# Twelve modulation vectors of a two-block network made by GpSimd and ScalarE in the feed forwards, in place of TensorE

## The chip, the core and the metric

The kernel runs on one core of a Trainium2 chip. The metric is device time in microseconds. Engines are named as the profile names them: PE is TensorE's matmul, PEld its weight load, DVE is VectorE, ACT is ScalarE, POOL is GpSimd, SP issues most DMAs. Each engine runs its own instructions in the order in which the program emits them; semaphores order them across engines.

## What is computed

A latent stream of 512 tokens and a context stream of 256 tokens, 1024 features each, pass two layers of a first block (attention, then a feed forward; a gated linear recurrence, then a feed forward) and two layers of a second block. Every norm is modulated by vectors that depend on a conditioning alone, one conditioning for each stream:

```python
mod_lat = jnp.dot(jax.nn.silu(c), ada_w[layer]) + ada_b[layer]
mod_ctx = jnp.dot(jax.nn.silu(c_ctx), ada_w[layer]) + ada_b[layer]
sh1, sc1, gt1, sh2, sc2, gt2 = jnp.split(mod_lat, 6, axis=-1)
...
x = x + gt1 * out_lat
x = x + gt2 * conv_ffn(modulate(rmsnorm(x, norm2_g[layer]), sh2, sc2), ...)

def conv_ffn(h, w_up, conv_w, conv_b, w_down):
    gate, val = jnp.split(jnp.dot(h, w_up), 2, axis=-1)
    return jnp.dot(jax.nn.silu(dwconv(gate, conv_w, conv_b)) * val, w_down)
```

The second block has three such vectors a layer (`w_mod`). That is 18 vectors of 1024 features, for two streams each; each is a product of a conditioning of 1024 with a matrix of 1024 x 1024. In the last layer of each block the context isn't updated, and some vectors are needed for the latents alone.

## The kernel before

Features lie over the 128 partitions (8 tiles, `KT`), tokens along the free axis (768 columns: context 256, latents 512). All products are exact float32 products made of three single passes: an operand is split into a high part (ACT, `split`, L357 to L360) and a low part (DVE, L360 through `tt`, L346). Weights come in tiles of 128x1024 (`raw`, three buffers, SP, L383); `weight` (L400) hands out the parts of one tile, loads up to three ahead and splits one ahead (tiles `wh` and `wl`).

`blk` (L510) is one block: take a weight, multiply 8 K tiles in three passes (`lin`, L409), call `fill`, then `tick`, then queue the evacuation of this block. `later` (L429) queues a function for a later `tick`; functions due at the same tick run in the order of their third argument. So the evacuation of a block is emitted behind the products of the next one.

A feed forward (`ffn`, L898) runs over 22 pairs of up blocks (gate, value). The gate's evacuation is `put` (DVE from PSUM), `conv` (L844, one `tensor_scalar` and four `scalar_tensor_tensor`), a tanh on ACT and the SiLU product on DVE; the value's is a product from PSUM, one or two `scalar_tensor_tensor`, and the split of the result (tiles `ah`, `ahl`). After each group of 2 or 3 pairs, beginning one pair late, the down products follow: 8 output tiles, with a `fill` after every second one (L962). The feed forward of layer 0 has both streams, that of layer 1 the latents alone, so that its blocks are a third shorter.

Modulation vectors are queued as steps in `self.todo`: 8 steps a vector, one for each tile of 128 rows of the matrix. A step of `modvec` (L532) is four matmuls of 128x32 by 128x256 in float32 (two passes each) into one PSUM bank, from a tile `ada` of 512 KB (two buffers) that SP loaded two steps ahead. After the eighth step ACT evacuates the bank, PE turns it by two transposes (L555) and DVE adds the bias. `fill(n)` (L646) runs up to n queued steps if `self.quota` allows; `mod(name)` (L669) runs what is missing when a vector is wanted. `run` (L2309) sets the quota by stage: 24 steps in the first attention, 48 in feed forward 0, 24 in feed forward 1, 16 and 16 in the second block. POOL is used for sums of squares and some products in other stages, not in the middle of the feed forwards.

Of the kernel before, what the change touches and what calls it, by code (L numbers as in the profile page):

```python
# [30 lines left out]
WIDE = {2: 512, 3: 256}       # columns of a tile of the second weights, by the K tiles of a chunk  # L31
# [3 lines left out]
# ---------------------------------------------------------------- host layout  # L35
# [19 lines left out]


def _vec(v):
    """[n * 128] -> [128, n]."""
    return v.reshape(-1, 128).T

# [13 lines left out]
def _constants():  # L74
# [7 lines left out]
    for b in range(5):                      # 3..7: two 64-lane heads of a block  # L82
        m = np.zeros((128, 32))
        m[:64, 2 * b] = 1 / 64
        m[64:, 2 * b + 1] = 1 / 64
        s.append(m)
    for q in range(8):                      # 8..15: 96 lanes of a head
# [7 lines left out]
    for p in range(4):                      # 16..19: nope lanes of a pair of heads  # L95
# [4 lines left out]
    m = np.zeros((128, 32))                 # 20: shared rotary lanes of the keys  # L100
    m[:32, :8] = 1 / 96
    s.append(m)
    for q in range(4):                      # 21..24: all lanes into column q
        m = np.zeros((128, 32))
        m[:, q] = 1 / 128
        s.append(m)
# [5 lines left out]
    fold = np.zeros((128, 2))               # adds the rows 32 g + v over g  # L112
# [4 lines left out]
    cos, sin = _rope_angles(8)              # [32, 512]  # L117
# [5 lines left out]
    cos, sin = _rope_angles(16)             # [64, 512]  # L123
# [3 lines left out]
    low = np.where(i[None, :] <= i[:, None], 0.0, NEG)   # [t, s]: s <= t  # L127
# [17 lines left out]
def _prepare(inp):  # L145
    """Arrays of the launch: inputs laid out for the chip, and constants of the shapes."""
# [5 lines left out]
    o["ada"] = a["ada_w"]  # L152
    o["mod"] = a["w_mod_2"]
# [92 lines left out]
# ---------------------------------------------------------------- the program  # L246

ALLB = ((0, 0, 512), (512, 512, 258))        # (psum column, operand column, n); the last two are the shifts
# [3 lines left out]
ORDER = (6, 7, 4, 5, 0, 1, 2, 3)              # of the tiles of a merge  # L252
SC, SL = (0, NC), (NC, T)                    # column ranges of ctx and lat
# [3 lines left out]
class _Halves(list):  # L257
    """A weight tile in column halves: w[:, a:b] within one of them."""
# [8 lines left out]
class _Kernel:  # L267
    """The program in issue order: each engine runs its instructions in the order they are emitted."""

    def __init__(self, ctx, tc, I, at, out):  # L270
# [15 lines left out]
        self.quota, self.log = 0, False  # L286

    def split_psum(self, a, at=0):
        """Two tiles of two banks, and four of one bank or, for a == 3, a third large one and two;
        at: the place of the next large tile in their cycle, the third one the last."""  # L290
# [13 lines left out]
    # ---- tiles  # L304
# [26 lines left out]
    # ---- engines  # L331
# [4 lines left out]
    def logs(self):  # L336
        """The activation table that has the logarithm."""
# [19 lines left out]
    def split(self, hi, lo, x):  # L357
        """x as the sum of two parts that single passes carry."""
        self.act(hi, x)
        self.tt(lo, x, hi.bitcast(F32), ALU.subtract)  # L360

    def parts(self, t, c, name="hi"):
        """The two parts of t[:, c]."""
# [4 lines left out]
    # ---- weights, in the order of their use  # L368
# [31 lines left out]
    def weight(self, name, i):  # L400
        """The parts of the next weight tile; the following ones are loaded and split ahead."""
# [7 lines left out]
    def lin(self, w, xs, segs, off=0, stride=128):  # L409
        """psum[:, ...] = w^T x over the K tiles xs, three single passes a product."""  # L410
# [17 lines left out]
    # ---- work that follows a product once the next one is under way  # L428
# [17 lines left out]
    def lead(self, specs, h, segs, pre):  # L446
        """The first products of a phase, K tile by K tile as pre(k) makes the tiles; evacuated at once."""
# [21 lines left out]
    def pair(self, specs, xs, pre=None):  # L469
        """Two products side by side, their last K tiles at the end, or K tile by K tile behind pre."""  # L470
# [19 lines left out]
    def begin(self, specs, h, pre=None, streams=None):  # L490
        """The first two products of a phase; they are evacuated during the next one, when the inverse
        rms is there."""
# [25 lines left out]
    # ---- modulation vectors  # L518
    def cond(self, names, key):
        """silu of the two conditionings as a zero-padded stationary operand."""  # L520
# [9 lines left out]
        return S  # L530

    def modvec(self, name, S, w, c0, bias):  # L532
# [33 lines left out]
        for k in range(KT):  # L566
            self.todo.append((lambda k=k: load(k), lambda k=k: step(k)))

    def first_mods(self, S, w, c_sc, c_sh, b_sc, b_sh, g, h, consts, after):
        """Scale and shift of the first phase, feature tile by feature tile, and its scaled residual."""  # L570
# [75 lines left out]
    def fill(self, n=1):  # L646
        """n eighths of a pending vector, the loads two ahead."""
        def load():
            for i in range(min(self.ahead, len(self.todo))):
                if self.todo[i][0]:  # L650
                    self.todo[i][0]()
                    self.todo[i] = (None, self.todo[i][1])

        for _ in range(min(n, self.quota, len(self.todo))):
            self.quota -= 1
            load()
            self.todo.pop(0)[1]()
            load()

    def whole(self, flush=True):  # L660
        """Finish a vector that is under way."""
        if len(self.todo) % KT:
# [6 lines left out]
    def mod(self, name):  # L669
        while name not in self.mods:  # L670
            if name in self.coming:
# [6 lines left out]
    def gain(self, name, sc, g):  # L678
        """g * (1 + scale), per feature and stream."""
# [4 lines left out]
    # ---- norms  # L684
    def rows(self, ps, n):
        """[64, n] means -> their inverse roots."""
# [14 lines left out]
    def heads(self, ps, sel, sq, start, stop):  # L701
        """Means of heads into rows of two token halves."""
# [6 lines left out]
    def means(self, sqs, sel, streams):  # L709
        """Means over all lanes of the tiles: quarters of the tokens in partition groups, the same  # L710
        in each row of a group."""
# [8 lines left out]
    def root(self, ps, c0, n, load=True):  # L720
        """The inverse roots of means."""
# [10 lines left out]
    def refine(self, y, t, m, z):  # L732
        """y = m ** -0.5 with a Newton step."""
# [7 lines left out]
    def spread(self, R, f, streams=(0, 1)):  # L741
        """f(psum, stream, first column, end) with the token values spread over all lanes."""
# [10 lines left out]
    def rows_out(self, name, ps):  # L753
        """Inverse roots of heads, left in DRAM: [head, tokens]."""
# [7 lines left out]
    def row_in(self, d, rows):  # L762
        """The rows of one head, or of two heads over the lane halves, spread over the lanes."""
# [6 lines left out]
    def start(self, A, sh, lat=False):  # L770
        """State of a normalized, modulated residual: scaled residual and shift in parts, K tile by
        K tile; the inverse rms multiplies the products."""
# [23 lines left out]
    def accumulate(self, acc, x, c, alone=False):  # L796
        """Squares of x into the list of sums."""
# [7 lines left out]
    def arm(self, h, streams=None):  # L805
        """Inverse rms: the sums after the next product, the spread after the one behind it."""
# [16 lines left out]
    def put(self, ps, h, lat=None):  # L823
        """psum * rstd + shift product."""
# [6 lines left out]
    def scaled(self, ps, h, lat):  # L831
        """The terms of put: psum * rstd, shift product."""
# [6 lines left out]
    def times(self, out, t, b, y, lat):  # L839
        """(t + b) * y."""  # L840
# [3 lines left out]
    def conv(self, src, w, b, lat):  # L844
        """Three taps along the tokens of each stream."""
# [8 lines left out]
    def silu2(self, x, c):  # L854
        """2 * silu, in place."""
# [1544 lines left out]
```

## Time and profile before

| | |
|---|---|
| time, median of 3 runs | 2530.7 us (2529.43 to 2530.71) |
| span of the profiled execution | 2526.1 us |
| PE / PEld | 97% / 81% of the span |
| DVE / ACT / POOL | 61% / 39% / 9% |
| mean granted clock of TensorE | 0.989 of full speed |
| DMA | 238.55 MB, 94 GB/s in the mean |

The time includes a few microseconds around the span. PE's busy time includes the tails of pipelined matmuls, so it is read here by the spacing of starts. A line such as L346 or L343 is a helper that many places call; the names of the tiles (output, then inputs) tell which place it is. An instruction's record begins when its engine takes it up; where it then waits for something inside the chip, the wait is part of its duration.

### The profile page before, as it was taken

Reading aid. Unit: us, or ns where it says so; the run is one execution under the profiler, and the core shown is the slowest. Engines: PE = TensorE matmul, PEld = TensorE weight load, DVE = VectorE, ACT = ScalarE, POOL = GpSimd, SP = SyncE. Lnnn points to the kernel's source line nnn. Section 1 sums busy time; section 2 is a strip of 40 time slices with the busy share of each in tenths; the row PEclk is TensorE's granted clock in tenths of the full one; section 3 lists DMA queues with packets and bytes.
Section 4 is the critical chain, followed back from the end, with each engine's and each line's share of the span. In section 5 each row is a group of like instructions: output and inputs, shape, how many; then the busy total and the mean of one; then the engine's idle time right before and its main releaser. Section 6 shows DMA issues by size and latency. Waiting matters only on the chain.

```text
span 2526.1 us, 40542 instructions
## 1 busy us (share of the span) xinstructions
PE 2456.3 (97%) x16338; PEld 2049.2 (81%) x16338; DVE 1551.3 (61%) x2736; ACT 973.2 (39%) x2217; POOL 215.4 (9%) x149
## 2 busy tenths in 40 slices
PE   7998999999999999998999999999999999989998
PEld 5776666887888888887889888999878778879797
DVE  4436876556555656667666566666745575266764
ACT  4226666322121222243445422333432473344563
POOL 2001232100000000012110100000110000130001
PEclk9999999999999999998999999999999999999999
DMA  8441110124334322113121255332223202333012
GB/s 284 151 152 46 32 63 30 61 90 142 120 122 126 109 83 76 53 57 109 59 80 62 81 196 167 99 95 97 86 95 134 76 2 84 101 105 101 18 47 88
DMA packets 82731, 238.55 MB, mean 94 GB/s; under 512 B 10032, under 2 KB 22256, under 8 KB 82544
## 3 DMA queue, kind: packets, MB, share of 16 engines
q1 hardware_dynamic: 82256, 235.90, 29.0%
q8 instruction: 129, 2.11, 0.4%
q14 instruction: 58, 0.48, 0.1%
q10 hardware_dynamic: 288, 0.07, 0.0%
HBM read 233.27 MB, written 2.66 MB: 93 GB/s over the span
## 4 chain that ended last, share of the span: by engine, by line
PE 88%; DVE 6%; ACT 2%; DMA 2%; issue 1%; POOL 0%; SPq 0%; DVEq 0%; ACTq 0%; POOLq 0%
PE A L355 71%; PE B L355 14%; PE B L1077 3%; DMA ada<-in_ada_dram 1%; DVE sm L1066 1%; DVE wl L346 1%; DVE kf L346 1%; ACT P L334 0%; DVE conv L343 0%; DVE hl L343 0%; ACT wh L334 0%; DMA stsel<-in_stat_dram 0%; ACT hh L334 0%; DVE y L346 0%; DMA raw<-in_w_in_dram 0%
## 5 line engine op out<-in xcount | busy, mean ns | idle before, releaser
L355 PE MATMUL A<-hh,wh 128*128 128x258 f32 (+2 forms) x2704 | 646.5, 320 | 13.1 <-ACT hh L334 3.8
L355 PE MATMUL A<-hl,wh 128*128 128x258 f32 (+2 forms) x2704 | 631.1, 315 | 2.9 <-DVE hl L343 2.9
L346 DVE TENSOR_TENSOR wl<-raw,wh 128x512 fp32r<-128x512 f32 (+2 forms) x546 | 377.1, 713 | 417.1 <-ACT wh L334 401.8
L355 PE MATMUL A<-hh,wl 128*128 128x258 f32 (+2 forms) x2704 | 630.3, 314 | 0.0
L334 ACT ACTIVATE wh<-raw 128x512 fp32r<-128x512 f32 (+2 forms) x546 | 318.8, 604 | 567.8 <-PE A L355 399.7
L355 PEld LDWEIGHTS A<-hh,wh 128*128 128x128 f32 x2704 | 419.3, 190 | 75.0 <-issue 13.9
L355 PEld LDWEIGHTS A<-hl,wh 128*128 128x128 f32 x2704 | 419.2, 190 | 36.5 <-DVE hl L343 4.1
L355 PEld LDWEIGHTS A<-hh,wl 128*128 128x128 f32 x2704 | 419.3, 190 | 33.3
L346 POOL TENSOR_TENSOR sq<-sq 128x768 f32<-128x768 f32 (+2 forms) x45 | 65.5, 1454 | 1204.4 <-ACT sq L334 599.7
L334 ACT ACTIVATE P<-A,sm 128x768 f32<-128x768 f32 (+3 forms) x176 | 127.9, 727 | 97.1 <-DVE sm L1066 91.3
L355 PE MATMUL A<-ah,wh 128*128 128x512 f32 (+1 forms) x528 | 163.1, 363 | 1.2 <-DVE x L343 1.1
L355 PE MATMUL A<-ah,wl 128*128 128x512 f32 (+1 forms) x528 | 159.7, 357 | 0.0
L355 PE MATMUL A<-ahl,wh 128*128 128x512 f32 (+1 forms) x528 | 159.3, 356 | 0.0
L1066 DVE TENSOR_REDUCE sm<-A 128x1 f32<-128x768 f32 (+3 forms) x176 | 129.2, 734 | 45.0 <-PE A L355 44.2
L343 DVE SCALAR_TENSOR_TENSOR x<-A,gt2h,x 128x512 f32<-128x512 f32 x192 | 119.7, 655 | 43.4 <-PE A L355 43.3
L1077 PE MATMUL B<-ident,P 128*128 128x128 f32 x768 | 124.7, 287 | 7.6 <-DVE pt L1080 2.5
L1077 PEld LDWEIGHTS B<-ident,P 128*128 128x128 f32 x768 | 84.0, 143 | 51.3 <-issue 21.6
L334 ACT ACTIVATE th<-conv 128x768 f32<-128x768 f32 (+1 forms) x52 | 38.4, 739 | 221.1 <-DVE conv L343 221.1
L343 DVE SCALAR_TENSOR_TENSOR conv<-put,small,conv 128x511 f32<-128x511 f32 (+1 forms) x168 | 110.3, 670 | 5.0
L355 PEld LDWEIGHTS A<-ah,wh 128*128 128x128 f32 x528 | 86.8, 188 | 26.9 <-issue 4.6
L346 DVE TENSOR_TENSOR put<-A,rbc 128x768 f32<-128x768 f32 (+1 forms) x111 | 93.2, 840 | 21.4 <-ACT sm L334 21.3
L355 PE MATMUL B<-ada,S 128*32 128x256 f32 x1152 | 91.3, 397 | 9.1 <-DMA ada<-in_ada_dram 8.9
(356 smaller groups left out, 3328.9 us busy)
## 6 DMA issues: line engine op xcount, KB each, us to landing
raw<-in_w_up_dram SPq DMA_DIRECT2D x88, 512.0 KB, 3.3
raw<-in_w_in_dram SPq DMA_DIRECT2D x81, 512.0 KB, 3.9
ada<-in_ada_dram SPq DMA_DIRECT2D x80, 512.0 KB, 4.1
ada<-in_mod_dram SPq DMA_DIRECT2D x48, 512.0 KB, 3.9
raw<-in_w_dn_dram SPq DMA_DIRECT2D x48, 384.0 KB, 3.2
raw<-in_w_o_dram SPq DMA_DIRECT2D x24, 512.0 KB, 4.3
ada<-in_ada_dram SPq DMA_DIRECT2D x16, 384.0 KB, 8.0
raw<-in_w_dn_dram SPq DMA_DIRECT2D x8, 512.0 KB, 5.7
```

The costliest lines, as they stand in the source:

```text
L334: return self.nc.scalar.activation(out, in_, f, **k)
L343: return self.nc.vector.scalar_tensor_tensor(out, x, sc, y, op0=op0, op1=op1)
L346: return (e or self.nc.vector).tensor_tensor(out, x, y, op=op)
L355: return self.nc.tensor.matmul(out, l, r, start=start, stop=stop)
L1066: nc.vector.tensor_reduce(g.nm[:, z], u.ps[:, cols], axis=AX.X, op=ALU.max, negate=True)
L1077: nc.tensor.transpose(ps[:, 128 * i:128 * i + 128], u.P[:, c:c + 128], self.ident)
```

## The change

Six vectors of layer 1 of the first block (`sc1`, `sh1`, `gt1`, `sc2`, `sh2`, `gt2`) and all six of the second block are made by a new `modrow` in place of `modvec`. The matrices are stored transposed, so that a tile has 128 output features over the partitions and the 1024 inputs along the free axis. The conditioning is written once to DRAM (four DMAs of S's columns, behind the first attention), and loaded back as a row spread over all partitions. A step multiplies the tile by the row on POOL (`tensor_tensor`, once for each stream that needs the vector), and ACT sums along the free axis with `accum_out`. With two streams the first product goes to a spare tile and the second is made in place; with one it is made in place.

```diff
+    def rows_of(self, key):
+        if self.rowt is None:
+            self.rowt = [None, [self.pt(n=D) for _ in range(2)], self.pt(n=D)]
+        if self.rowt[0] != key:
+            self.rowt[0] = key
+            for v in range(2):
+                self.nc.sync.dma_start(self.rowt[1][v], self.sd[key][v:v + 1].to_broadcast([128, D]))
+        return self.rowt[1:]
+
+    def modrow(self, name, key, w, n, bias):
+        nc, st = self.nc, {}
+        def load(k):
+            st[k] = self.pw["ada"].tile([128, 1024], F32, tag="ada", name="ada")
+            nc.sync.dma_start(st[k], w[k])
+        def step(k):
+            rows, spare = self.rows_of(key)
+            if k == 0:
+                st["m"] = self.const("m_" + name, [128, KT, 2])
+                if n == 1:
+                    nc.gpsimd.memset(st["m"], 0.0)
+            m, raw = st["m"], st.pop(k)
+            outs = [spare, raw][2 - n:]
+            for v, o in enumerate(outs):
+                self.tt(o, raw, rows[v], ALU.mult, nc.gpsimd)
+            self.pending = True
+            def sums():
+                for v, o in enumerate(outs):
+                    self.act(o, o, accum_out=m[:, k, v:v + 1])
+                self.pending = False
+                if k == KT - 1:
+                    self.tt(m[:, :, 0:n], m[:, :, 0:n], bias..., ALU.add, nc.gpsimd)
+                    self.mods[name] = m
+            self.later(sums, 1, 3)
```

The sums are queued for the next `tick` with the third argument 3, so they are emitted behind the evacuations due at that tick. While such a step is pending, `fill` doesn't begin another and doesn't load ahead; a `fill` runs one such step at most. While the row tiles exist, `split` makes the low part by another DVE instruction:

```diff
     def split(self, hi, lo, x):
         self.act(hi, x)
-        self.tt(lo, x, hi.bitcast(F32), ALU.subtract)
+        if self.rowt:
+            self.stt(lo, x, 1.0, hi.bitcast(F32), ALU.mult, ALU.subtract)
+        else:
+            self.tt(lo, x, hi.bitcast(F32), ALU.subtract)
```

In `fill`, and in `run`:

```diff
             for i in range(min(self.ahead, len(self.todo))):
-                if self.todo[i][0]:
-                    self.todo[i][0]()
-                    self.todo[i] = (None, self.todo[i][1])
+                f, g, row = self.todo[i]
+                if f and not (row and i and self.pending):
+                    f()
+                    self.todo[i] = (None, g, row)
         for _ in range(min(n, self.quota, len(self.todo))):
+            row = self.todo[0][2]
+            if row and self.pending:
+                return
             self.quota -= 1
             load()
             self.todo.pop(0)[1]()
+            if row:
+                return
             load()
...
+        for j, n, v in ((1, "sc1", 2), (0, "sh1", 2), (2, "gt1", 1), (4, "sc2", 1), (3, "sh2", 1), (5, "gt2", 1)):
+            self.modrow(f"{n}_1", 0, I["ada1"][j], v, self.s("ada_b1", 8 * j, 8))
         for l in range(2):
             for j, n in ((1, "s_sc"), (0, "s_sh"), (2, "s_gt")):
-                self.modvec(f"{n}_{l}", S2, I["mod"][l], 1024 * j, self.s(f"mod_b{l}", 8 * j, 8))
+                self.modrow(f"{n}_{l}", 1, I[f"mod{l}"][j], 1 if l and j == 2 else 2, self.s(f"mod_b{l}", 8 * j, 8))
...
+        for d, S in zip(self.sd, (S1, S2)):
+            for v in range(2):
+                nc.sync.dma_start(d[v].rearrange("(k p) -> p k", p=128), S[:, :, v])
-        self.quota = 48
+        self.quota = 72
         h = self.ffn(0, h, orders[0], norm("a1", self.s("n1g1", 0, KT), "sc1_1", "sh1_1"))
         h = self.odd(h, norm("f1", self.s("n2g1", 0, KT), "sc2_1", "sh2_1", True))
-        self.quota = 24
+        self.quota = 32
```

So the quota of feed forward 0 is 8 steps of `modvec` (`gt2_0`), 16 row steps for two streams, 32 for one, 16 for two; that of feed forward 1 is 24 row steps for two streams and 8 for one. No steps are left for the second block. `ffn` gives the row tiles back at its end (`self.rowt = None`). The rest of the diff takes comments out.

## Rows read from the trace of the kernel before

**Rows 1.** The page, part 1: busy us, share of the span, instructions.
```profile
PE 2456.3 (97%) x16338; PEld 2049.2 (81%) x16338; DVE 1551.3 (61%) x2736; ACT 973.2 (39%) x2217; POOL 215.4 (9%) x149
```

**Rows 2.** Stretches of feed forward 0 and 1: busy us (instructions) by engine, clock, DMA.
```profile
core 0: us, PE busy (x) PEld busy (x) DVE busy (x) ACT busy (x) POOL busy (x), PEclk, DMA share, GB/s
560.00:900.00 340.00, 339.40 (x2094) 275.12 (x2093) 196.45 (x327) 68.71 (x132) 0.00 (x0) 1.00 0.41 129
...
1455.00:1566.00 111.00, 109.89 (x878) 92.22 (x877) 72.03 (x117) 29.94 (x65) 0.00 (x0) 1.00 0.60 196
```

**Rows 3.** Timeline of PE, modulation steps: start us, us, engine, line, operation, tiles, form.
```profile
747.40 0.64 PE L355 MATMUL B<-ada,S 128*32 128x256 f32 x8
756.60 0.64 PE L355 MATMUL B<-ada,S 128*32 128x256 f32 x8
...
1455.35 1.07 PE L355 MATMUL B<-ada,S 128*32 128x256 f32 x16
...
1498.19 0.64 PE L355 MATMUL B<-ada,S 128*32 128x256 f32 x8
1504.69 0.64 PE L355 MATMUL B<-ada,S 128*32 128x256 f32 x8
```

**Rows 4.** Timeline of DVE, feed forward 0 without steps: the SiLU product of two pairs.
```profile
1003.90 0.96 DVE L343 SCALAR_TENSOR_TENSOR conv<-th,conv 128x768 f32<-128x768 f32 x1 [0.91 <-ACT th L334]
...
1020.73 0.96 DVE L343 SCALAR_TENSOR_TENSOR conv<-th,conv 128x768 f32<-128x768 f32 x1 [0.92 <-ACT th L334]
```

**Rows 5.** POOL's groups by form: count, busy us, mean ns, idle before, releasers.
```profile
L346 POOL TENSOR_TENSOR kl<-kf,kh 128x768 fp32r<-128x768 f32 x8 | 14.7, 1833 | 23.0 <-ACT kh L334 21.2 <-PE B L1077 1.7
...
L346 POOL TENSOR_TENSOR y<-y,x 128x512 f32<-128x512 f32 x3 | 3.8, 1276 | 0.2
```

**Rows 6.** Timelines of DVE and ACT, feed forward 1: evacuation of gate, then value.
```profile
1499.38 0.68 DVE L346 TENSOR_TENSOR put<-A,rbc 128x512 f32<-128x512 f32 x1
...
1502.78 0.63 ACT L334 ACTIVATE th<-conv 128x512 f32<-128x512 f32 x1 [4.04 <-DVE conv L343]
...
1507.28 0.68 DVE L346 TENSOR_TENSOR val<-A,rbc 128x512 f32<-128x512 f32 x1
...
1508.79 0.63 ACT L334 ACTIVATE ah<-val 128x512 fp32r<-128x512 f32 x1 [2.17 <-DVE val L343]
```

**Rows 7.** The same in feed forward 0.
```profile
739.24 0.95 DVE L346 TENSOR_TENSOR put<-A,rbc 128x768 f32<-128x768 f32 x1
...
744.22 0.85 ACT L334 ACTIVATE th<-conv 128x768 f32<-128x768 f32 x1 [5.56 <-DVE conv L343]
...
750.25 0.95 DVE L346 TENSOR_TENSOR val<-A,rbc 128x768 f32<-128x768 f32 x1
...
752.42 0.84 ACT L334 ACTIVATE ah<-val 128x768 fp32r<-128x768 f32 x1 [2.83 <-DVE val L343]
```

**Rows 8.** ACT's groups by form: reading an accumulator.
```profile
L334 ACT ACTIVATION_READ_ACCUMULATOR P<-A,sm 128x1 f32 x176 | 34.2, 195 | 0.0
```

**Rows 9.** Timelines of DVE and POOL: four taps alone, and both at once.
```profile
741.73 2.46 DVE L343 SCALAR_TENSOR_TENSOR conv<-put,small,conv 128x511 f32<-128x511 f32 x4
...
1172.14 4.03 DVE L343 SCALAR_TENSOR_TENSOR conv<-put,small,conv 128x511 f32<-128x511 f32 x4
...
1172.65 1.27 POOL L346 TENSOR_TENSOR pt<-pt,wl 128x512 f32<-128x512 f32 x1 [17.32 <-DMA pt<-cb]
...
1269.97 1.16 POOL L346 TENSOR_TENSOR pt<-pt,wr 128x512 f32<-128x512 f32 x1 [0.30 <-DMA pt<-cb]
1270.14 3.25 DVE L346 TENSOR_TENSOR hu<-hu,sm 128x512 f32<-128x512 f32 x2
...
1271.10 3.44 POOL L346 TENSOR_TENSOR pt<-pt,conv 128x512 f32<-128x512 f32 x2
1273.31 1.78 DVE L346 TENSOR_TENSOR wl<-raw,wh 128x512 fp32r<-128x512 f32 x1
```

**Rows 10.** DMA issues: bytes each and median us to landing.
```profile
ada<-in_ada_dram SPq DMA_DIRECT2D x80, 512.0 KB, 4.1
```

**Rows 11.** A stretch of the first attention, columns as in rows 2.
```profile
175.00:190.00 15.00, 12.76 (x68) 9.37 (x67) 5.58 (x11) 3.24 (x6) 0.00 (x0) 0.89 0.60 179
```

More of the change, by code (lines that the diff above doesn't have):

```diff
@@ L151, in _prepare @@
     o["cT"] = np.ascontiguousarray(a["ctx_2"][0].T.reshape(KT, 128, NC))
-    o["ada"] = a["ada_w"]
-    o["mod"] = a["w_mod_2"]
+    o["ada"] = a["ada_w"][0]
+    lanes = lambda w: np.ascontiguousarray(w.T.reshape(-1, KT, 128, D))
+    o["ada1"] = lanes(a["ada_w"][1])
+    for l in range(2):
+        o[f"mod{l}"] = lanes(a["w_mod_2"][l])
     blk = lambda s, n: [np.arange(s + 128 * i, s + 128 * i + 128) for i in range(n)]
@@ L286, in __init__ @@
         self.quota, self.log = 0, False
+        self.rowt, self.pending = None, False
     def split_psum(self, a, at=0):
@@ L530, in cond @@
         return S
+    def rows_of(self, key):
[27 more added lines that the diff above has]
+                if k == KT - 1:
+                    self.tt(m[:, :, 0:n], m[:, :, 0:n], bias.rearrange("p (k o) -> p k o", o=1).to_broadcast([128, KT, n]), ALU.add, nc.gpsimd)
+                    self.mods[name] = m
+            self.later(sums, 1, 3)
+        for k in range(KT):
+            self.todo.append((lambda k=k: load(k), lambda k=k: step(k), True))
     def modvec(self, name, S, w, c0, bias):
@@ L566, in modvec @@
         for k in range(KT):
-            self.todo.append((lambda k=k: load(k), lambda k=k: step(k)))
+            self.todo.append((lambda k=k: load(k), lambda k=k: step(k), False))
     def first_mods(self, S, w, c_sc, c_sh, b_sc, b_sh, g, h, consts, after):
@@ L657, in fill @@
             self.todo.pop(0)[1]()
+            if row:
+                return
             load()
     def whole(self, flush=True):
-        if len(self.todo) % KT:
+        if len(self.todo) % KT and not self.todo[0][2]:
             n = len(self.todo) % KT
@@ L670, in mod @@
         while name not in self.mods:
-            if name in self.coming:
+            if name in self.coming or self.pending:
                 self.tick()
@@ L963, in ffn @@
         self.flush()
+        self.rowt = None
         return nxt
@@ L2321, in run @@
         S2 = self.cond(("c_2", "c_ctx_2"), "2")
-        for l in range(2):
-            for j, n in ((1, "sc1"), (0, "sh1"), (2, "gt1"), (4, "sc2"), (3, "sh2"), (5, "gt2")):
-                if l or j > 1:
-                    self.modvec(f"{n}_{l}", S1, I["ada"][l], 1024 * j, self.s(f"ada_b{l}", 8 * j, 8))
+        for j, n in ((2, "gt1"), (4, "sc2"), (3, "sh2"), (5, "gt2")):
+            self.modvec(f"{n}_0", S1, I["ada"], 1024 * j, self.s("ada_b0", 8 * j, 8))
+        for j, n, v in ((1, "sc1", 2), (0, "sh1", 2), (2, "gt1", 1), (4, "sc2", 1), (3, "sh2", 1), (5, "gt2", 1)):
+            self.modrow(f"{n}_1", 0, I["ada1"][j], v, self.s("ada_b1", 8 * j, 8))
         for l in range(2):
             for j, n in ((1, "s_sc"), (0, "s_sh"), (2, "s_gt")):
-                self.modvec(f"{n}_{l}", S2, I["mod"][l], 1024 * j, self.s(f"mod_b{l}", 8 * j, 8))
+                self.modrow(f"{n}_{l}", 1, I[f"mod{l}"][j], 1 if l and j == 2 else 2, self.s(f"mod_b{l}", 8 * j, 8))
+        self.sd = [self.dr.tile([2, D], F32, tag=f"sd{i}", name=f"sd{i}") for i in range(2)]
         self.plan_even()
@@ L2364, in run @@
         h = self.start(self.const("A_a0", [128, KT, 2]), self.const("m_sh1_0", [128, KT, 2]))
-        pre = self.first_mods(S1, I["ada"][0], 1024, 0, self.s("ada_b0", 8, 8), self.s("ada_b0", 0, 8), self.s("n1g0", 0, KT), h, consts, after)
+        pre = self.first_mods(S1, I["ada"], 1024, 0, self.s("ada_b0", 8, 8), self.s("ada_b0", 0, 8), self.s("n1g0", 0, KT), h, consts, after)
         self.quota = 24
         h = self.even(h, pre, norm("f0", self.s("n2g0", 0, KT), "sc2_0", "sh2_0"))
-        self.quota = 48
+        for d, S in zip(self.sd, (S1, S2)):
+            for v in range(2):
+                nc.sync.dma_start(d[v].rearrange("(k p) -> p k", p=128), S[:, :, v])
+        self.quota = 72
         h = self.ffn(0, h, orders[0], norm("a1", self.s("n1g1", 0, KT), "sc1_1", "sh1_1"))
         h = self.odd(h, norm("f1", self.s("n2g1", 0, KT), "sc2_1", "sh2_1", True))
-        self.quota = 24
+        self.quota = 32
         h = self.ffn(1, h, orders[1], norm("s0", self.s("gpre0", 0, KT), "s_sc_0", "s_sh_0"))
```

## The prediction

> **What bounds the kernel now.** I read the page's busy shares first [rows 1]: TensorE is busy 97% of the span. So work taken from it is worth its full time wherever nothing else comes due in its place. Second, the stretches by engine [rows 2]: in the two feed forwards PE is busy without a break at full clock, DVE for 58% (196.45 of 340 us) and 65% (72.03 of 111 us), ACT for 20% and 27%, GpSimd (POOL) for nothing; it looks free. Third, the timeline of PE, to see what one modulation step costs there [rows 3]. Last, what DVE does while POOL works, which decides the forecast and is shown where it is used.
>
> **What is removed.** 96 steps (12 vectors of 8) leave TensorE; before, 40 of them ran in feed forward 0, 24 in feed forward 1, 32 in the second block. In feed forward 0 an up block with a step recurs after 756.60 - 747.40 = 9.20 us [rows 3]; without one, a pair of blocks recurs after 1020.73 - 1003.90 = 16.83 us (read at DVE's SiLU product), 8.42 a block [rows 4]. One step is 0.78 us. In feed forward 1 the spacing is 6.50 us [rows 3], so a block alone is 5.72. Where two steps are issued together they last 1.07 us and not 0.64 [rows 3]: the second adds 0.43, a double costs 1.21.
> Feed forward 0: 40 x 0.78 = 31. Feed forward 1: 4 doubles and 16 singles, 4.8 + 12.5 = 17. Second block: 4 doubles and 18 singles, 4.8 + 14 = 19; its last 6 steps lie in waits for a norm, and I count 1.5 for them. The 24 transposes and the evacuations take some 2. Sum 71 us, all of it on the path, since PE has no idle time there.
>
> **What is added.** 152 POOL products of 128x1024 (96 in feed forward 0, 56 in feed forward 1) and as many ACT sums; 12 additions and 5 memsets of 16 columns on POOL, too small to count; four row loads in feed forward 0 and two in feed forward 1, and four writes of 4-byte elements to DRAM on SP.
> A POOL product: the trace has none this wide. 768 columns take 1833 ns and 512 take 1276 ns [rows 5]: 2.18 ns a column, so 2.39 us for 1024. I take 2.4, and 2.3 to 2.6 as bounds (in proportion to the row of 512 it would be 2.55). A page gives a price too. The Trainium skill, "GPSIMD Engine Reference", section 3.1, has 4497 ns for 2048 columns of such an operation, so by estimate 2.25 us; a two-vector step would then hold POOL for 4.5 us, not 4.8, and the loss below would shrink by some 0.3 us a step, 15 us in all.
> An ACT sum: 0.63 us for 512 and 0.85 for 768 columns [rows 6, 7] give 1.07 for 1024, and 0.195 for reading the accumulator [rows 8]: 1.25 us. ACT has the room; its order matters.
>
> **POOL keeps DVE out.** In the chain of four convolution taps, all from SBUF, DVE takes 2.46 us alone, and 4.03 us where one POOL product of 1.27 us and the start of another fall into it [rows 9]. The other rows show the form of it: two POOL products (3.44 us for both, 1.16 for the one ahead of them) and two DVE products (3.25 us for both) take turns, one at a time; the DVE split that starts at 1273.31 ends at 1275.09, 0.55 us after POOL's end at 1274.54, as if it had done its start beforehand and all of its columns afterwards. I found no DVE instruction with two SBUF inputs that began under a POOL product and ended before it, unless POOL itself was the one that waited. The exchange of `tensor_tensor` for `scalar_tensor_tensor` in the split doesn't help, since the taps are that instruction.
> The Trainium skill, "SBUF — State Buffer", section "Summary: rules for kernel authors", speaks against this change: with two SBUF inputs on DVE and a GpSimd operation that reads SBUF, the second to start waits for the whole of the first. The trace agrees, by the 0.55 us above; by that rule rival 2 below has only the work split in advance to live on.
>
> **A two-vector step as a chain.** ACT runs in order: splits of the next weight, the evacuation of the block before (its tanh, or the high part of the product), then this step's sums. POOL's first product of the next step writes the spare tile that the first sum has just read, so a step can't begin before that sum. From there: product 2.4; DVE's first low part 0.55; POOL's second product, which has queued meanwhile, 2.4; the second low part 0.55; together 5.9 us. Then DVE's evacuation up to ACT's end, and the first sum, 1.25. The evacuation takes, in feed forward 1, from 1499.38 to 1503.41 = 4.0 us for a gate block and 1507.28 to 1509.42 = 2.1 for a value block [rows 6]; in feed forward 0, 739.24 to 745.07 = 5.8 and 750.25 to 753.26 = 3.0 [rows 7].
> A pair in feed forward 1: (5.9 + 4.0 + 1.25) + (5.9 + 2.1 + 1.25) = 20.4 us, and PE needs 11.4. In feed forward 0: 13.0 + 10.2 = 23.2 us, PE needs 16.83. So PE waits for weights: 9.0 and 6.3 us a pair. This wait is new; behind ACT's sums queue the next weight's high parts, behind these DVE's low parts, behind these PE.
> One-vector steps multiply in place and don't wait for the sum. In feed forward 0 they fit (some 16.4 us a pair); in feed forward 1 I add 2 us a pair.
> Down products, two output tiles a step. From 8.42 / 24 and 5.72 / 24 us for a K tile of three passes, PE needs 4.2 (two K tiles) or 6.3 us in feed forward 0, 2.9 or 4.3 in feed forward 1. A two-vector step needs two products, 4.8, and with two `ada` buffers sum, load (4.1 to land [rows 10]) and start, about 5.5 us.
>
> **The sum.** Steps fall in order of the fills. Feed forward 0 has 9 up pairs with two-vector steps, 9 x 6.3 = 57; 8 steps in short downs, 8 x 1.3 = 10; the first row load and the change of the rows, during which SP waits for POOL, 5; less what PE and the split weights hold in advance, about 7 us in each of two runs, 14: +58. Feed forward 1 has 7 such pairs, 63; downs 8 x 2.6 + 2 x 1.2 = 23; one-vector pairs 6; row load 3; less 6: +89. The small writes to DRAM cost nothing: three weights lie loaded ahead; without that cover some 10 us.
> +147 - 71 = +76. Against the profiled execution, 2526.1 us of span and 4.6 around it (it stands at the median of 2530.7), that is 2607; with the advance somewhat larger and POOL at 2.3, 2600, which I forecast. Bounds: at 2.3 us, with half of the waits met by work elsewhere, +25; at 2.6, with no advance, +110.
>
> **Rivals.** (1) DVE and POOL use each other's idle time, and only the sum of their busy time counts. Feed forward 1 from its second pair to the end of its steps is some 153 us of PE; 56 products take 134. DVE is busy for 65% of the 171 us that this takes before, 111; without its evacuations and additions from PSUM (some 0.7 us each, 44 of them) 80. 134 + 80 less 153 and the advance of 6: +55. The same count gives +20 in feed forward 0. 75 - 71 leaves 2535 (2515 to 2560). For it: DVE has gaps while it waits for ACT. Against it: the order above ties POOL to the end of each evacuation.
> (2) The waits are absorbed, PE stays fed, the gain stays: 2531 - 71 = 2460 (to 2510). For it: the busy shares [rows 2] and the block of advance of the splits. Against it: [rows 9].
> (3) PE's clock falls in its new idle time. In the window with 2.2 us of idle the granted clock was 0.89, in the feed forwards 1.00 [rows 2, 11]. At the lower level (1.2 GHz) a pair of feed forward 1 would take PE 22.9 us, more than the chain's 20.4; if that held throughout, 7 x 2.5, and 9 x 10 in feed forward 0: up to 2700; it begins to decide once more than two thirds of a stretch are at the lower level.
> That steps are left over and run late in a row isn't likely: feed forward 0 has 70 fills for 64 row steps, feed forward 1 has 74 for 32.
>
> **How the numbers follow.** Forecast (chain) 2600, 0.63; rival 1, 0.19, half of it on each side; rival 2, 0.13; rival 3, 0.05. Range 2510 to 2640: it leaves out most of rivals 2 and 3. The forecast's own range is 2556 to 2640. A run of this kernel tells 0.2% from no change: faster 0.21, same 0.04, slower 0.75.
>
> **What would show it.** After: DVE splits and taps in the first steps with means of 2 to 3 us; POOL products of 2.4 us, longer where DVE was first; PE idle in feed forward 1 released by ACT's and DVE's split; up pairs at 20 and 23 us with two vectors and at 17 with one; the second block shorter by 19 us. If PE is busy throughout both feed forwards, the chain is wrong and rival 2 holds. Wrong too if POOL runs steps ahead of ACT.

## The result, and the profile after

The changed kernel takes 2626.8 us (median of 4 runs, 2622.43 to 2629.46) where the kernel before takes 2530.1 beside it: ratio 1.0387, interval 1.0375 to 1.04. It is 97 us slower. The forecast was 2600, that is 70 slower, with a range from 2510 to 2640.

The page's busy line of the changed kernel, and its stretches (columns as in rows 2), answer to [rows 1, 2]. The stretches are: first steps with two vectors in feed forward 0, steps with one vector, the last steps with two vectors, the end of that feed forward; then feed forward 1 with two vectors, and after its last step.

```profile
PE 2430.5 (93%) x15546; PEld 2058.2 (79%) x15546; DVE 1747.1 (67%) x2712; ACT 1121.8 (43%) x2509; POOL 602.2 (23%) x318
```

```profile
560.00:720.00 160.00, 136.09 (x752) 115.75 (x751) 119.59 (x136) 60.73 (x117) 87.12 (x37) 0.94 0.34 118
720.00:985.00 265.00, 262.92 (x1485) 229.18 (x1484) 206.01 (x262) 87.00 (x170) 73.80 (x37) 0.99 0.37 126
985.00:1083.00 98.00, 81.89 (x435) 68.92 (x433) 69.53 (x72) 34.94 (x70) 44.90 (x20) 0.95 0.30 102
1083.00:1160.00 77.00, 60.68 (x305) 51.78 (x306) 65.17 (x79) 41.45 (x82) 49.60 (x26) 0.88 0.30 100
...
1566.00:1712.00 146.00, 111.24 (x688) 99.22 (x687) 114.30 (x106) 60.94 (x124) 86.55 (x37) 0.87 0.36 124
1760.00:1930.00 170.00, 170.00 (x1226) 161.00 (x1225) 122.73 (x204) 58.33 (x134) 6.19 (x6) 1.00 0.29 89
```

PE executes 792 instructions fewer and yet has lost its place as the bound: in every stretch with steps of two vectors it stands still for a seventh to a quarter of the time, with steps of one vector hardly, and after the last step not at all. No other engine is full there either. That is the mark of a chain, and the timelines of the changed kernel show it. First POOL, then DVE, then ACT, one pair of feed forward 1 (rows as in rows 3).

```profile
1575.22 2.36 POOL L350 TENSOR_TENSOR pt<-ada,pt 128x1024 f32<-128x1024 f32 x1 [5.61 <-ACT pt L338]
1577.66 2.69 POOL L350 TENSOR_TENSOR ada<-ada,pt 128x1024 f32<-128x1024 f32 x1
1584.07 2.41 POOL L350 TENSOR_TENSOR pt<-ada,pt 128x1024 f32<-128x1024 f32 x1 [3.72 <-ACT pt L338]
1586.56 2.69 POOL L350 TENSOR_TENSOR ada<-ada,pt 128x1024 f32<-128x1024 f32 x1
1594.85 2.35 POOL L350 TENSOR_TENSOR pt<-ada,pt 128x1024 f32<-128x1024 f32 x1 [5.61 <-ACT pt L338]
```

```profile
1571.90 1.54 DVE L347 SCALAR_TENSOR_TENSOR conv<-put,small,conv 128x511 f32<-128x511 f32 x2
...
1576.73 4.17 DVE L347 SCALAR_TENSOR_TENSOR wl<-raw,wh 128x512 fp32r<-128x512 f32 x2 [1.90 <-ACT wh L338]
1580.82 0.68 DVE L350 TENSOR_TENSOR val<-A,rbc 128x512 f32<-128x512 f32 x1
...
1585.59 4.20 DVE L347 SCALAR_TENSOR_TENSOR wl<-raw,wh 128x512 fp32r<-128x512 f32 x2 [1.91 <-ACT wh L338]
1589.71 0.68 DVE L350 TENSOR_TENSOR put<-A,rbc 128x512 f32<-128x512 f32 x1
```

```profile
1582.86 1.04 ACT L338 ACTIVATE pt<-pt 128x1024 f32<-128x1024 f32 x1
1583.81 0.19 ACT L338 ACTIVATION_READ_ACCUMULATOR pt<-pt 128x1 f32 x1
...
1593.64 1.04 ACT L338 ACTIVATE pt<-pt 128x1024 f32<-128x1024 f32 x1
```

Read it as a relay. POOL's two products and DVE's two low parts between them: 1575.22 to 1580.82, 5.60 us. The value's evacuation to ACT's first sum: to 1582.86, 2.04. The sum, until POOL begins the next step: to 1584.07, 1.21. Together 8.85 us. The gate block: 5.64, then 3.93, then 1.21, together 10.78. The pair is 19.6 us, and PE needs 11.4 of them. The two low parts take 4.17 us here, and 1.29 in a kernel below in which POOL writes as long but doesn't read.

By stage, read at the starts of ACT's tanh (tile `th<-conv`; first the kernel before, then the changed one, each the first and last pair of feed forward 0, the first tanh of the recurrence behind it, and the first and last of feed forward 1):

```profile
539.58 0.84 ACT L334 ACTIVATE th<-conv 128x768 f32<-128x768 f32 x1 [3.71 <-DVE conv L343]
...
1053.05 0.85 ACT L334 ACTIVATE th<-conv 128x768 f32<-128x768 f32 x1 [5.29 <-DVE conv L343]
...
1160.77 0.85 ACT L334 ACTIVATE th<-conv 128x768 f32<-128x768 f32 x1 [3.48 <-DVE conv L343]
...
1456.77 0.63 ACT L334 ACTIVATE th<-conv 128x512 f32<-128x512 f32 x1 [2.13 <-DVE conv L343]
...
1797.02 0.63 ACT L334 ACTIVATE th<-conv 128x512 f32<-128x512 f32 x1 [3.71 <-DVE conv L343]
```

```profile
536.15 0.84 ACT L338 ACTIVATE th<-conv 128x768 f32<-128x768 f32 x1 [3.71 <-DVE conv L347]
...
1075.74 0.84 ACT L338 ACTIVATE th<-conv 128x768 f32<-128x768 f32 x1 [8.55 <-DVE conv L347]
...
1205.23 0.85 ACT L338 ACTIVATE th<-conv 128x768 f32<-128x768 f32 x1 [3.48 <-DVE conv L347]
...
1503.47 0.64 ACT L338 ACTIVATE th<-conv 128x512 f32<-128x512 f32 x1 [2.14 <-DVE conv L347]
...
1912.99 0.63 ACT L338 ACTIVATE th<-conv 128x512 f32<-128x512 f32 x1 [3.72 <-DVE conv L347]
```

| stage | before | after | difference | forecast |
|---|---|---|---|---|
| to the first tanh | 539.6 | 536.1 | -3.4 | 0 |
| feed forward 0, its 22 pairs | 513.5 | 539.6 | +26.1 | +27 (58 - 31) |
| its end, to the recurrence's first tanh | 107.7 | 129.5 | +21.8 | 0 (in the row above) |
| recurrence | 296.0 | 298.2 | +2.2 | 0 |
| feed forward 1, its 22 pairs | 340.3 | 409.5 | +69.3 | +72 (89 - 17) |
| from there to the end (spans 2526.1 and 2620.3) | 729.1 | 707.4 | -21.8 | -19 to -22 |
| span | 2526.1 | 2620.3 | +94.2 | +76 |

Feed forward 1 came out as forecast. The agreement of the pairs of feed forward 0 is partly luck: the forecast had all 32 steps with two vectors of that feed forward in its pairs, and 8 of them ran behind its last tanh, in the next row, which was forecast at nothing and cost 22 us. The two rows together are +47.9 us, for +27.

### The profile page after: what moved, and what is told of

Read it like the earlier page. It is cut to its first block, busy times and chain, and to the rows that moved or that the text cites. A ratio compares the mean times of both kernels' runs of the same rounds, so it can differ in the third digit from the quotient of the medians.

```text
span 2620.3 us, 39530 instructions
## 1 busy us (share of the span) xinstructions
PE 2430.5 (93%) x15546; PEld 2058.2 (79%) x15546; DVE 1747.1 (67%) x2712; ACT 1121.8 (43%) x2509; POOL 602.2 (23%) x318
## 4 chain that ended last, share of the span: by engine, by line
PE 45%; DVE 9%; ACT 4%; issue 3%; POOL 2%; DMA 0%; ACTq 0%; DVEq 0%; SPq 0%; POOLq 0%
PE A L359 36%; PE B L359 7%; DVE wl L347 3%; PE B L1134 1%; DVE conv L347 1%; ACT pt L338 1%; ACT ada L338 1%; ACT wh L338 1%; POOL pt L350 1%; POOL ada L350 1%; DVE put L350 1%; DVE put L355 0%; DVE conv L356 0%; DVE hl L347 0%; DVE wl L350 0%
## 5 line engine op out<-in xcount | busy, mean ns | idle before, releaser
L359 PE MATMUL A<-hh,wl 128*128 128x258 f32 (+2 forms) x2704 | 639.2, 318 | 5.9 <-DVE wl L347 5.9
L359 PE MATMUL A<-hl,wh 128*128 128x258 f32 (+2 forms) x2704 | 637.6, 318 | 4.6 <-DVE hl L347 4.6
L359 PEld LDWEIGHTS A<-hh,wh 128*128 128x128 f32 x2704 | 427.2, 194 | 94.9 <-ACT wh L338 33.7
L359 PEld LDWEIGHTS A<-hh,wl 128*128 128x128 f32 x2704 | 425.9, 193 | 42.6 <-DVE wl L347 9.4
L347 DVE SCALAR_TENSOR_TENSOR wl<-raw,wh 128x512 fp32r<-128x512 f32 (+1 forms) x268 | 333.1, 1273 | 153.8 <-ACT wh L338 146.2
L350 DVE TENSOR_TENSOR wl<-raw,wh 128x512 fp32r<-128x512 f32 (+2 forms) x278 | 204.3, 761 | 231.5 <-ACT wh L338 227.3
L350 POOL TENSOR_TENSOR ada<-ada,pt 128x1024 f32<-128x1024 f32 x96 | 246.7, 2570 | 179.0 <-DMA ada<-in_ada_dram 140.4
L359 PE MATMUL A<-ah,wh 128*128 128x512 f32 (+1 forms) x528 | 170.3, 377 | 71.2 <-DVE val L350 54.0
L350 POOL TENSOR_TENSOR pt<-ada,pt 128x1024 f32<-128x1024 f32 x56 | 139.4, 2488 | 243.4 <-ACT pt L338 156.7
L359 PE MATMUL A<-ahl,wh 128*128 128x512 f32 (+1 forms) x528 | 165.7, 369 | 0.0
```

The costliest lines, as they stand in the source:

```text
L347: return self.nc.vector.scalar_tensor_tensor(out, x, sc, y, op0=op0, op1=op1)
L350: return (e or self.nc.vector).tensor_tensor(out, x, y, op=op)
L359: return self.nc.tensor.matmul(out, l, r, start=start, stop=stop)
```

## Experiments

The theory: POOL's products and DVE's instructions with two SBUF inputs take turns (while one of them runs, the other waits for its end), and in a step with two vectors this makes one chain with ACT's sums. Rivals: the loss is in the busy time of the two engines; in ACT's order alone; in what every step brings along, however many products it has; in the split's new instruction; in the place of the steps.

**Lost fills.** Where a `fill` follows a group of down products, it finds the last step still pending and returns; that fill is lost. The three steps that run late, at 1124, 1137 and 1150 us in the changed kernel, stand among POOL's sums of squares and DVE's splits for the next norm:

```profile
1124.38 2.79 POOL L350 TENSOR_TENSOR pt<-ada,pt 128x1024 f32<-128x1024 f32 x1
1127.26 2.44 POOL L350 TENSOR_TENSOR ada<-ada,pt 128x1024 f32<-128x1024 f32 x1
1130.09 1.98 POOL L350 TENSOR_TENSOR sq<-sq 128x768 f32<-128x768 f32 x1 [0.40 <-ACT sq L338]
...
1122.98 4.48 DVE L347 SCALAR_TENSOR_TENSOR wl<-raw,wh 128x512 fp32r<-128x512 f32 x2 [0.51 <-ACT wh L338]
...
1149.58 5.45 DVE L347 SCALAR_TENSOR_TENSOR hl<-x,A_a,hh 128x512 fp32r<-128x512 f32 x2
```

In this experiment such a `fill` emits the pending sums itself and goes on:

```diff
             if row and self.pending:
-                return
+                d = next(d for d in self.due if d[2] == 3)
+                self.due.remove(d)
+                d[1]()
```

> The changed kernel, but a fill that meets a step still pending emits that step's sums at once and goes on, where the changed kernel skips the fill. So no fill is lost behind a group of down products, and the 16 last steps of feed forward 0 end before its last 8 output tiles, in which the next phase is fed. If the tail of feed forward 0 (1083 to 1160 us of the changed kernel, where 3 steps lie between the sums of squares on POOL) is paid by these late steps, they cost 2.8 us each in an up block and not about 7: 2612 us (2602 to 2620). Rival: they cost the same wherever they lie: 2627 within 4 us.

Measured: 2619.4 us, ratio 1.0361 (1.0343 to 1.0378), at the upper edge of what was expected. The end of feed forward 0 shrank from 129.5 to 109.2 us, nearly that of before, but its 22 pairs took 546.7 in place of 539.6, and those of feed forward 1 414.5 in place of 409.5. The lost fills explain where the 22 us stood. They explain only some 7 us of the loss (the interval still touches that of the changed kernel, 1.0375 to 1.04): a step with two vectors costs nearly as much wherever it goes.

**Memsets in place of products.** Each product becomes three memsets of about the same time in all; the vectors are left out. Sums, waits, DMA transfers and POOL's time stay, the reading of SBUF by POOL goes (and so does the wait for the row loads).

```diff
-                self.tt(o, raw, rows[v], ALU.mult, nc.gpsimd)
+                for z in (D, D, 512):
+                    nc.gpsimd.memset(o[:, :z], 0.0)
```

> Each POOL product is replaced by three memsets of the same tile (1024, 1024 and 512 columns, by an estimate from the 732 ns of the memset of 768 columns about 2.4 us), which read nothing; the vectors are left out (zeros). Order, sums, loads and durations stay. Chain theory (products shut DVE out and the order carries it on): DVE's splits go back to about 0.75 us, a two-vector pair of feed forward 1 falls from 19.6 to 15.1 us (sum of the spare 1.25, two high parts 1.15, a low part 0.75, evacuation, sum 1.25; for gate and value 8.4 and 6.5), of feed forward 0 from 22.5 to 17.5; the time is 2510 us (2490 to 2535). Rival, the order of ACT alone: 2615 to 2630. Rival, only the exclusion matters: the pairs fall to 11.4 and 16.8, and the time to 2465.

Measured: 2510.4 us, ratio 0.9936 (0.9916 to 0.9956); pairs of 17.4 us in feed forward 0 and 14.8 in feed forward 1. Timelines of this kernel, POOL and DVE:

```profile
1503.97 2.55 POOL L567 MEMSET pt<- 128x1024 f32 x3 [0.94 <-ACT pt L338]
1506.46 2.71 POOL L567 MEMSET ada<- 128x1024 f32 x3
...
1505.51 1.29 DVE L347 SCALAR_TENSOR_TENSOR wl<-raw,wh 128x512 fp32r<-128x512 f32 x2 [1.91 <-ACT wh L338]
1506.72 0.68 DVE L350 TENSOR_TENSOR put<-A,rbc 128x512 f32<-128x512 f32 x1
1507.44 1.27 DVE L355 TENSOR_SCALAR put<-put,sm 128x512 f32<-128x512 f32 x1
```

With POOL just as busy (586.4 us against 602.2), the low parts take 1.29 us again, and the kernel is faster than before. Some 115 us lie between this kernel and the changed one, and what sets them apart is that POOL reads. Three smaller differences don't account for it. The wait for the row loads also goes, which the prediction priced at 8 us in all (5 and 3). The memsets are shorter than a product, at most 0.96 us in the mean, but a kernel below with pieces of 0.83 to 0.91 us that read still takes 2597 us. The vectors are left out in the next kernel too, which takes 2615. The Trainium skill, "SBUF — State Buffer", section "Who interferes with whom", says that a DVE instruction with two SBUF inputs contends with a GpSimd instruction that reads SBUF, not with one that only writes; the 4.17 and 1.29 us of the same two low parts agree.

**No sums.** ACT's sums are left out (and with them the vectors); products, loads and order stay.

```diff
-                for v, o in enumerate(outs):
-                    self.act(o, o, accum_out=m[:, k, v:v + 1])
```

> The changed kernel without ACT's sums (the vectors are left out, biases alone); POOL's products stay. Nothing ties POOL to ACT's order any more. Chain theory: what is left is the exclusion, counted by busy time alone, +55 in feed forward 1 and +20 in feed forward 0 against 71 saved: 2535 us (2515 to 2560). Rival, exclusion costs nothing without the order: 2460 to 2475. Rival, the exclusion alone makes the whole loss: 2615 to 2630.

Measured: 2615.0 us, ratio 1.035 (1.0329 to 1.0371), where the theory expected 2535: a clear miss. The theory had ACT's order as a link that the loss needs; it doesn't need it. Untied from ACT, POOL runs product after product, and DVE gets one instruction in behind each (timelines of this kernel, POOL and DVE):

```profile
1499.57 2.82 POOL L350 TENSOR_TENSOR pt<-ada,pt 128x1024 f32<-128x1024 f32 x1
1502.46 2.47 POOL L350 TENSOR_TENSOR ada<-ada,pt 128x1024 f32<-128x1024 f32 x1
1505.22 2.37 POOL L350 TENSOR_TENSOR pt<-ada,pt 128x1024 f32<-128x1024 f32 x1 [0.29 <-DMA ada<-in_mod_dram]
1507.67 2.66 POOL L350 TENSOR_TENSOR ada<-ada,pt 128x1024 f32<-128x1024 f32 x1
...
1500.79 1.88 DVE L355 TENSOR_SCALAR put<-put,sm 128x512 f32<-128x512 f32 x1
1502.70 2.51 DVE L356 TENSOR_SCALAR conv<-put,small 128x512 f32<-128x512 f32 x1
1505.25 5.63 DVE L347 SCALAR_TENSOR_TENSOR conv<-put,small,conv 128x511 f32<-128x511 f32 x2
```

Two taps that take 1.54 us otherwise take 5.63. A DVE instruction of 0.77 us with two SBUF inputs costs a whole product's time when products stand in line. The two `tensor_scalar` ahead of the taps, which read one large SBUF tile each, wait in the same way here: 1.88 and 2.51 us, for 0.49 and 0.55 alone. So these rows count the price in turns: number of such DVE instructions that meet a product, times the length of a product. ACT's sums even hold the products apart.

**The split by `tensor_tensor`.** The exchange of the split's instruction is undone.

```diff
     def split(self, hi, lo, x):
         self.act(hi, x)
-        if self.rowt:
-            self.stt(lo, x, 1.0, hi.bitcast(F32), ALU.mult, ALU.subtract)
-        else:
-            self.tt(lo, x, hi.bitcast(F32), ALU.subtract)
+        self.tt(lo, x, hi.bitcast(F32), ALU.subtract)
```

> The split of the changed kernel by tensor_tensor as before, not by scalar_tensor_tensor. Chain theory: behind a POOL product both end 0.55 us after it, and elsewhere DVE isn't the bound: 2624 us (2616 to 2629). Rival, the exchange spares DVE or POOL waits: over 2632.

Measured: 2624.6 us, ratio 1.0392 (1.0374 to 1.0411). That is the changed kernel's time within the noise (1.0387): the exchange is worth nothing.

**One vector a step.**

```diff
-        nc, st = self.nc, {}
+        nc, st, n = self.nc, {}, 1
```

> Every row step makes the latents' vector alone: one GpSimd product of 128x1024 and one sum a step, 96 products in place of 152. The context's part of the vectors is left out, so this is a measure of cost and no other kernel. By the theory of turns (each GpSimd product costs DVE one turn, and a step of two products costs two of them in a chain with ACT's sum) the pairs of feed forward 1 take 14.8 us in place of 19.6, those of feed forward 0 at most 18 in place of 22.4, and the tail of feed forward 0 loses nothing: 2506 us (2492 to 2522). If the loss lay in something that each step brings, however many products it has (the pending rule, the row loads, SP's order), the kernel would keep more than half of its 95 us: over 2570.

Measured: 2519.5 us, ratio 0.9974 (0.9964 to 0.9984), in the upper part of the expected range; most of the loss doesn't come with the step as such. Pairs of feed forward 1 with steps took 14.5 to 14.8 us (one 17.4). By the ratios, with 2528 us for the kernel before, the 56 second products and what goes with them (a second sum each, and the wait for the spare tile) cost 0.0413 x 2528 = 104 us, 1.9 us each. The first ones cost less: if 71 us leave TensorE, 2528 - 71 = 2457, and 0.9974 x 2528 = 2521 is 64 us above that, 0.67 us for each of 96 products, a little under the 0.74 us (71 / 96) that a step frees.

**Products in two halves, and in four.** The columns stay the same, the instructions get shorter.

```diff
-                self.tt(o, raw, rows[v], ALU.mult, nc.gpsimd)
+                for z in (slice(0, 512), slice(512, D)):
+                    self.tt(o[:, z], raw[:, z], rows[v][:, z], ALU.mult, nc.gpsimd)
```

> Each product is issued in two halves of 512 columns, some 1.28 us each, the same columns in all. If DVE gets in once between two GpSimd instructions, whatever their length (turns), it gets twice as many turns in a step: a two-vector pair of feed forward 1 falls from 19.6 to some 17.8 us, one of feed forward 0 from 22.4 to some 20.6, and the time to 2600 us (2585 to 2612). If the loss goes by busy time or by the port, halves cost their extra start and no more: 2627 to 2637.

> As with halves, but each product in four pieces of 256 columns. By the rows of 512 and 768 columns a piece takes some 0.72 us, so a product 2.87 us in place of 2.55 (halves) and 2.34 (whole). If what counts is only how many times DVE gets in, the time falls again by about as much as from whole to halves, to 2565 to 2580. If a turn costs what the GpSimd piece in it lasts, the wait of a turn falls by 0.56 us this time after 1.06 us the time before, and the longer products take about that much back: 2588 (2575 to 2605). If GpSimd's starts dominate: over 2605.

Measured: halves 2595.0 us, ratio 1.0276 (1.0262 to 1.029); quarters 2597.0 us, 1.0266 (1.0249 to 1.0283). A pair of feed forward 1 falls from 19.6 to 18.3 and 17.4 us, one of feed forward 0 from 22.4 to 20.6 and 20.2. The products themselves grow: POOL's busy time over all of them is 386 us whole (246.7 + 139.4), 446 in halves, 514 in quarters (groups of POOL by form: whole, halves, quarters):

```profile
L350 POOL TENSOR_TENSOR ada<-ada,pt 128x1024 f32<-128x1024 f32 x96 | 246.7, 2570 | 179.0 <-DMA ada<-in_ada_dram 140.4 <-DMA ada<-in_mod_dram 31.2 <-ACT sm L338 3.0
L350 POOL TENSOR_TENSOR pt<-ada,pt 128x1024 f32<-128x1024 f32 x56 | 139.4, 2488 | 243.4 <-ACT pt L338 156.7 <-DMA pt<-sd 86.7
```

```profile
L350 POOL TENSOR_TENSOR ada<-ada,pt 128x512 f32<-128x512 f32 x192 | 299.8, 1581 | 150.5 <-DMA ada<-in_ada_dram 113.1 <-DMA ada<-in_mod_dram 21.3 <-ACT wh L338 6.9
L350 POOL TENSOR_TENSOR pt<-ada,pt 128x512 f32<-128x512 f32 x112 | 146.5, 1328 | 198.5 <-ACT pt L338 111.8 <-DMA pt<-sd 86.1 <-DMA ada<-in_mod_dram 0.6
```

```profile
L350 POOL TENSOR_TENSOR ada<-ada,pt 128x256 f32<-128x256 f32 x384 | 335.9, 906 | 122.3 <-DMA ada<-in_ada_dram 104.1 <-DMA ada<-in_mod_dram 14.1 <-ACT ah L338 4.1
L350 POOL TENSOR_TENSOR pt<-ada,pt 128x256 f32<-128x256 f32 x224 | 178.2, 827 | 176.6 <-ACT pt L338 89.3 <-DMA pt<-sd 86.5 <-DMA ada<-in_mod_dram 0.6
```

More work on POOL and a kernel that is 28 us faster: the loss doesn't go by POOL's busy time. From halves to quarters nothing more is gained, which rules out that only the number of times counts that DVE gets in (2565 to 2580 by that). The pairs go on falling, but nothing is won elsewhere: the end of feed forward 0 takes 129.7 us after 125.3. What takes the gain back wasn't separated; the profiled execution with quarters also holds a long wait, shown at the end, and took 12 us more than the median.

**Only four vectors by POOL.** gt1, sc2, sh2 and gt2 of layer 1, each wanted for the latents alone, all in feed forward 0; the other eight stay on TensorE as before. Then the same with halves.

```diff
-            self.modrow(f"{n}_1", 0, I["ada1"][j], v, self.s("ada_b1", 8 * j, 8))
+            if v == 2:
+                self.modvec(f"{n}_1", S1, I["ada"][1], 1024 * j, self.s("ada_b1", 8 * j, 8))
+            else:
+                self.modrow(f"{n}_1", 0, I["ada1"][j], v, self.s("ada_b1", 8 * j, 8))
...
-                self.modrow(f"{n}_{l}", 1, I[f"mod{l}"][j], 1 if l and j == 2 else 2, self.s(f"mod_b{l}", 8 * j, 8))
+                self.modvec(f"{n}_{l}", S2, I["mod"][l], 1024 * j, self.s(f"mod_b{l}", 8 * j, 8))
...
-        self.quota = 72
+        self.quota = 56
...
-        self.quota = 32
+        self.quota = 16
```

> Only the four vectors of layer 1 that are wanted for the latents alone (gt1, sc2, sh2, gt2) are made by GpSimd, all of them in feed forward 0, where a pair has 16.8 us of TensorE's work and a step of one product fits; the other eight go back to TensorE, in the places of the kernel before. 32 steps of 0.78 us leave TensorE, 25 us; the one-vector pairs of the changed kernel measured 16.9 to 18.1 us where TensorE needs 16.83, so 16 pairs give back 5 to 12 us, the row load and its gap up to 5. Turns: 2515 us (2504 to 2526), faster than the kernel before. If every GpSimd product costs its 0.78 us or more wherever it stands, 2530 or more.

> The four latent vectors alone by GpSimd, eight by TensorE, each product in two halves of 512 columns. With whole products this kernel lost some 12 us of the 25 that leave TensorE, about 5 of them at the row load, which stays; halves should give back half of the rest: 2508 us (2502 to 2514). If what it loses has nothing to do with turns: 2511 to 2517, as with whole products.

Measured: 2512.2 us, ratio 0.9941 (0.9928 to 0.9955), and with halves 2507.5 us, 0.9913 (0.9899 to 0.9928). Both beat the kernel before, the second by 22 of the 25 us that 32 steps free. Feed forward 0 with its end takes 610.8 and 605.1 us where it took 621.2; if its 24 freed steps (gt2 stood in feed forward 1 before) cost nothing else it would take 602.5. So 32 steps of one vector cost some 8.4 us there with whole products, and 2.6 with halves (one execution of each; the first is 4 us above its median). One stretch of the second kernel:

```profile
720.00:985.00 265.00, 265.00 (x1511) 231.81 (x1510) 189.29 (x259) 85.22 (x167) 82.34 (x61) 1.00 0.33 121
```

POOL works for 82 us of it, more than in the changed kernel, and PE doesn't stand still.

## Why the prediction was right

**What leaves TensorE.** The second block, where nothing is added, is 21.8 us shorter, forecast 19 to 22. Right.

**Prices.** A product takes 2.35 to 2.41 us where it starts first and 2.7 to 2.8 where DVE was first; forecast 2.4; the other price that the prediction gave, 2.25, is too short. A sum takes 1.04 us and 0.19 for the accumulator; forecast 1.25. Right. But the sum had come to 2607, and it was lowered to 2600 with POOL at 2.3 and a larger advance: that step went the wrong way.

**POOL keeps DVE out.** Right, and read from two places of the kernel before [rows 9]. In the first of them the prediction saw one POOL product and the start of another; the second lies within the four taps whole (timeline of POOL, kernel before), which changes nothing in the argument:

```profile
1174.48 1.41 POOL L346 TENSOR_TENSOR pt<-pt,wl 128x512 f32<-128x512 f32 x1 [0.56 <-DMA pt<-cb]
```

The low parts take 4.2 us for two, and the memsets show that reading is the cause. That the exchange in the split doesn't help was right too. What the prediction leaves out is that `tensor_scalar` from SBUF to SBUF waits as well, as the kernel without sums shows.

**The chain.** Two vectors: 5.6, 2.04 or 3.93, and 1.21 us were measured for 5.9, 2.1 or 4.0, and 1.25; pairs of 19.6 and 22.4 us for 20.4 and 23.2. Feed forward 1 came out at +69 for +72. The pieces are right. (For the down products the prediction calls 8.42 / 24 us a K tile of three passes; that is one pass. The 4.2 and 6.3 us that follow are right.) The reason that the prediction gave against rival 1, that ACT's order ties POOL down, was not the one that counts: without the sums the loss remains, 2615 us where a budget of busy time gives at most 2560. That excludes rival 1, and the turns in which DVE gets in are what its budget lacked.

**Steps of one vector in feed forward 0.** The prediction said that they fit, at 16.4 us a pair. Pairs took 16.9 to 19.5. The kernel with only these steps puts their price at 8 us, with the row load, which the prediction had counted by itself (5 us for both). Mis-sized by the rest.

**Steps left over.** This sentence failed: "feed forward 0 has 70 fills for 64 row steps". It counts fills, but a pending step makes the `fill` behind each group of downs return. Steps slid, and three with two vectors fell into the end of the feed forward, among the next norm's work. With the fills given back the kernel is 7 us faster. These 7 and a part of the 8 above are over half of the 18 us by which the sum (+76) fell short of the span (+94.2). By the stages the shortfall lies in feed forward 0 with its end, +47.9 for +27; with the fills given back it is still +34.7. What makes up the rest wasn't resolved.

**Rivals 2 and 3.** Absorbed: no, PE stood still as the chain says. It is near the truth only for steps of one vector in feed forward 0. The clock: granted 0.87 to 0.95 where PE waits, but the pairs of feed forward 1 stayed at 19.6 us, and their length is made up of POOL's, DVE's and ACT's pieces; the 22.9 us of that rival were not reached. At a mean of 0.87 PE would need 11.4 / 0.87 = 13.1 us of such a pair, by estimate, so it isn't the bound there. (The two thirds of a stretch at which the clock was to decide come out of the prediction's own numbers as 0.88 in feed forward 1 and 0.55 in feed forward 0; a mean of 0.87 is 0.26 at the lower level.) No run tested the clock by itself.

## What to carry over

An engine that is idle in the busy line isn't free if its instructions and a busy engine's keep each other waiting: count how many of the other's instructions meet one of its own, and charge each of these the length of what it waits for. Before work is moved to GpSimd, look for stretches where VectorE has slack for a whole such instruction (here a block of 8.4 us took one product nearly for free, and not two), move only what fits there, and try it in shorter instructions: halves of 1.3 us gained 28 us here, quarters nothing more. When steps are spread over slots, count the slots that a rule takes away, not those that exist.

## What was not expected of the hardware

A memset on POOL, which reads nothing, leaves DVE's instructions with two SBUF inputs alone (1.29 us for two low parts), but a `tensor_scalar` from SBUF to SBUF beside it took 1.27 us, at 1507.44, in place of 0.49.

DVE doesn't always get its turn. In the profiled execution of the kernel with quarters, two low parts of DVE took 15.77 us, while POOL ran the 20 pieces from 582.70 to 596.37 at their undisturbed length, 2.76 us for four (timelines of DVE and POOL):

```profile
581.74 15.77 DVE L347 SCALAR_TENSOR_TENSOR wl<-raw,wh 128x512 fp32r<-128x512 f32 x2 [6.16 <-ACT wh L338]
...
582.70 2.76 POOL L350 TENSOR_TENSOR ada<-ada,pt 128x256 f32<-128x256 f32 x4
585.43 2.76 POOL L350 TENSOR_TENSOR pt<-ada,pt 128x256 f32<-128x256 f32 x4
...
593.61 2.76 POOL L350 TENSOR_TENSOR ada<-ada,pt 128x256 f32<-128x256 f32 x4
```

PE waited 18.5 us for what followed. That execution took 2609.4 us where the median of the five is 2597.0. Halves at the same place let DVE in behind the second piece (2.97 us for the two low parts). It was seen once; what decides who comes next wasn't tried.
